# Squares of the new x summed on TensorE tile by tile, and element-wise work taken off GpSimd

## The chip, the cores and the metric

The kernel runs on one core of one Trainium2 chip. What is counted is device time in microseconds (us) of one execution, as the median of several runs. The engines are named as the profile names them: PE is TensorE's matrix product, PEld its weight load, DVE is VectorE, ACT is ScalarE, POOL is GpSimd, SP is the engine that issues most transfers.

## The reference

A decoder trunk of two layers, with 512 tokens and a width of 1024, all in f32. Layer 0 mixes with dilated attention and a state-space model (S5), layer 1 ("odd") with a gated linear recurrence. Each layer then has a gated feed-forward network (FFN) with 2816 hidden columns. Every one of the four sub-layers is put between two RMS norms:

```
for layer in range(2):
    hn  = rms_norm(x, norm_mix_pre[layer])
    mix = even_mixer(hn, ...) if layer == 0 else odd_mixer(hn, ...)
    x   = x + rms_norm(mix, norm_mix_post[layer])
    hn  = rms_norm(x, norm_ffn_pre[layer])
    ff  = (silu(hn @ w_gate) * (hn @ w_up)) @ w_down
    x   = x + rms_norm(ff, norm_ffn_post[layer])

rms_norm(x, g) = x * rsqrt(mean(x * x, axis=-1) + 1e-6) * g

odd_mixer: z = xn @ w_in; xc = conv4(z[:, :1024]) + bias
    gate_r, gate_i = sigmoid(xc @ w_r + b_r), sigmoid(xc @ w_i + b_i)   # blocks of 256
    log_a = -8 * gate_r * softplus(-lam)
    h[t]  = exp(log_a) * h[t-1] + sqrt(-expm1(2 * log_a)) * (gate_i * xc)
    y     = (h * gelu(z[:, 1024:])) @ w_out
```

## The kernel before

The activations lie transposed: x is eight tiles `xT[f]` of 128 channels by 512 tokens, and a product of a weight with x gives 128 output columns by 512 tokens in a PSUM bank. Each f32 operand is split into a high and a low part, so that one product is three matmuls: hi·hi, hi·lo and lo·hi (`mm3`, whose matmuls all carry line 170). The parts of a weight are `whi_` (a copy on ACT, line 240) and `wlo_` (a subtraction, line 241, on DVE unless `wrows` or `first_cols` is given another engine); those of the normed x are `xh_` (ACT, line 499) and `xl_` (DVE, line 487).

The sum over channels in a norm is a sum over partitions. `col_sums` takes it as matmuls with one column of ones: 128 tokens come out as one PSUM column. `rstd_of` turns the four columns into 1/rms: a scale on DVE (`rst`, line 378), a power on POOL (`rsy`, line 381), and, where the next norm wants it, `eps` on DVE (line 383). `bcast_sb` spreads the result over the partitions with four 128x128 matmuls (`bc`) and a copy into SBUF (`bcs`).

Four times the kernel goes through `out_proj`: products with an output matrix (`op_`), the RMS norm after it, and the addition to x. The tail of it runs by halves of 256 tokens (`norm_half`): for each f the output is scaled (line 492), added to `xT[f]` (DVE for f = 0, POOL for the others, lines 496 and 498), copied to `xh`, and subtracted for `xl`. Between these steps PE already makes the first four column blocks of the next stage (`half_cols`, banks `mo0b`, `fd0b`, `mo1b`) with x that is not yet divided by its rms. In this tail the order is pinned as it is written (`seq_of`, `pe.pin`). Everywhere else a scheduler at build time sets the order on each engine; on the chip an engine then runs its list in that order.

What the next stage needs is 1/rms of the new x, and this is `pre_rstd`: eight squares of whole tiles on ACT (`sq_`, line 423, two buffers), six additions into two accumulators `sqacc_` (line 425; f under 4 on DVE, the others on POOL), eight one-column products `cs_`, and `rstd_of`. In `ffn_up` the function `mid` calls it after the products of the first pair of columns that is built by a scheme with seven products over half tiles instead of eight (`product`; banks `f00b` to `f03b` with the pair's number at the end, 84 matmuls of 128x256 each; weight sums on DVE, lines 629 to 632; sums of x on DVE, lines 651 to 654, with hi and lo parts `th_`, `tl_`). The four early column blocks are copied out unscaled (line 614) and multiplied once the factor is there. In the odd layer `mid` runs while the first columns go through the convolution.

In the odd layer, per tile f: convolution with hi and lo (`ch`, `cl`, line 1512), gates (`gr`, `gi`, line 1541; `xc` times `gi` on POOL, line 1542), exp and tanh (`ga`, `gr`, lines 1549 and 1550), `lm` = `ga` squared on POOL (line 1556), `gr` (line 1557), a square root on ACT, `gr` times `xc`, the scan (line 1561), the gelu branch `gg` (lines 1574 to 1583; `gt` is its square, on POOL, line 1576), and `y1h`, `y1l` (line 1587), which the products `op_mo` of the odd layer read.

Of the kernel before, what the change touches and what calls it, by code (L numbers as in the profile page):

```python
# [94 lines left out]
def hybrid_trunk(  # L95
# [318 lines left out]
    def pre_rstd(nm, keep=None):  # L414
        accs = []
        for f in (0, 4, 1, 5, 2, 6, 3, 7):
            eng = dve if f < NF // 2 else pool
            if f % (NF // 2) == 0:
                accs.append(sb.tile([P, S], F32, tag="sqacc", bufs=2, name=f"sqacc_{nm}{f}"))
                act.activation(accs[-1], xT[f], AF.Square)  # L420
            else:
# [1 line left out]
                act.activation(q, xT[f], AF.Square)
# [1 line left out]
                eng.tensor_tensor(acc, acc, q, op=ALU.add)  # L425
        return rstd_of(col_sums(lambda t: [a[:, t * P:(t + 1) * P] for a in accs], 0, NT, nm, "mid"), NT, nm,
                       keep=keep)

    def out_proj(wget, ks, yh, yl, pname, layer, nm, otile, gname, glayer, ntail, tail_alloc, early, eng0=None,
# [42 lines left out]
        ready.clear()  # L472

        def norm_half(h):
# [15 lines left out]
            for f in range(NF):  # L490
# [8 lines left out]
                seq_of(act.activation(xh[f][:, HS[h]], xf, AF.Copy, scale=col(gname, glayer * NF + f)))  # L499
# [971 lines left out]
    def odd_body(xh, xl, first, lp):
# [52 lines left out]
        def gates(blk):  # L1524
# [4 lines left out]
            for n in range(2):  # L1529
# [12 lines left out]
                pool.tensor_tensor(xc[f], xc[f], t, op=ALU.mult)  # L1542
# [121 lines left out]
```

## Time and profile before

| | |
|---|---|
| median of 3 runs | 1211.34 us (1208.27 to 1212.36) |
| the profiled execution | 1211.84 us |
| its span in the trace | 1210.1 us |
| mean granted PE clock | 0.973 |
| POOL busy | 181.9 us, 173 instructions |

The trace shows the stages at about these times: attention and S5 to 200 us, out-projection of layer 0 with its norm to 293, FFN of layer 0 up to 513 and down to 642, its norm to 667, odd layer to 801, its out-projection with its norm to 854, FFN of layer 1 up to 1073, its down product to the end.

In the rows below, "128x512 f32 x8" is the shape of an instruction and how often it stands in the group. In rows of the timeline the first number is the start, the second the duration; several instructions may be merged into one row (x4). In square brackets is how long the engine was idle before it, and what it then came free on. In rows of a table of windows there are for each engine the busy time in the window and the number of instructions, then the granted clock of PE (1.00 is full), the share of the DMA engines that was busy, and GB/s.

### The profile page before, as it was taken

Reading aid. Unit: us, or ns where it says so; the run is one execution under the profiler, and the core shown is the slowest. Engines: PE = TensorE matmul, PEld = TensorE weight load, DVE = VectorE, ACT = ScalarE, POOL = GpSimd, SP = SyncE. Lnnn points to the kernel's source line nnn. Section 1 sums busy time; section 2 is a strip of 40 time slices with the busy share of each in tenths; the row PEclk is TensorE's granted clock in tenths of the full one; section 3 lists DMA queues with packets and bytes.
Section 4 is the critical chain, followed back from the end, with each engine's and each line's share of the span. In section 5 each row is a group of like instructions: output and inputs, shape, how many; then the busy total and the mean of one; then the engine's idle time right before and its main releaser. Section 6 shows DMA issues by size and latency. Waiting matters only on the chain.

```text
span 1210.1 us, 19987 instructions
## 1 busy us (share of the span) xinstructions
PE 1138.7 (94%) x7406; PEld 1012.8 (84%) x7406; DVE 905.5 (75%) x1823; ACT 622.9 (51%) x1255; POOL 181.9 (15%) x173
## 2 busy tenths in 40 slices
PE   7899999999699999999999999599799999999997
PEld 6787766888699999988889878389689999988886
DVE  7978775369789998983327897977989998894224
ACT  6555576448455545652334467354755455482222
POOL 2000020432400000000135045434310000000001
PEclk9899899999799999999999999799999999999999
DMA  8344410712233323332331223140243233343321
GB/s 207 103 137 128 110 47 1 192 36 70 70 96 105 89 79 105 107 108 94 120 96 36 87 88 105 53 135 6 69 122 97 84 100 89 105 131 105 97 69 70
DMA packets 165273, 113.44 MB, mean 94 GB/s; under 512 B 26820, under 2 KB 141752, under 8 KB 165176
## 3 DMA queue, kind: packets, MB, share of 16 engines
q1 hardware_dynamic: 161848, 109.94, 30.9%
q10 hardware_dynamic: 3040, 2.17, 0.7%
q8 instruction: 58, 0.95, 0.3%
q14 instruction: 39, 0.32, 0.1%
q0 software_dynamic: 288, 0.07, 0.0%
HBM read 103.75 MB, written 4.19 MB: 89 GB/s over the span
## 4 chain that ended last, share of the span: by engine, by line
PE 57%; DVE 6%; issue 5%; ACT 3%; DMA 3%; POOL 2%; SPq 0%; DVEq 0%; POOLq 0%; ACTq 0%
PE op_fd L170 10%; PE fo L170 10%; PE f00b L170 4%; PE f01b L170 4%; PE f02b L170 4%; PE f12b L170 4%; PE f10b L170 4%; PE f11b L170 4%; PE op_mo L170 2%; PE f03b L170 2%; PE f13b L170 2%; PE fd0b L170 2%; POOL sqacc_f L425 2%; PE xbb L170 2%; PE mo1b L170 1%
## 5 line engine op out<-in xcount | busy, mean ns | idle before, releaser
L241 DVE TENSOR_TENSOR wlo_fo<-wraw_fo,whi_fo 128x512 fp32r<-128x512 f32 x44 | 30.3, 691 | 64.0 <-PE fo L170 58.1
L170 PE MATMUL op_fd<-hi_f,whi_fd 128*128 128x512 f32 (+1 forms) x200 | 73.5, 368 | 0.0
L170 PE MATMUL op_fd<-lo_f,whi_fd 128*128 128x512 f32 (+1 forms) x200 | 73.2, 366 | 0.0
L170 PE MATMUL op_fd<-hi_f,wlo_fd 128*128 128x512 f32 (+1 forms) x200 | 72.9, 368 | 0.0
L241 DVE TENSOR_TENSOR wlo_fd<-wraw_fd,whi_fd 128x512 fp32r<-128x512 f32 x44 | 30.6, 705 | 55.2 <-ACT whi_fd L240 41.1
L170 PE MATMUL fo<-wlo_fo,hi_f 128*128 128x512 f32 x176 | 69.6, 396 | 0.0
L170 PE MATMUL fo<-whi_fo,lo_f 128*128 128x512 f32 x176 | 69.2, 394 | 0.0
L170 PE MATMUL fo<-whi_fo,hi_f 128*128 128x512 f32 x176 | 68.8, 395 | 0.0
L240 ACT ACTIVATE whi_fo<-wraw_fo 128x512 fp32r<-128x512 f32 x44 | 27.3, 631 | 71.4 <-DMA wraw_fo<-in_ffn_w_down_dram 45.1
L240 ACT ACTIVATE whi_fd<-wraw_fd 128x512 fp32r<-128x512 f32 x44 | 27.3, 630 | 56.4 <-DMA wraw_fd<-in_ffn_w_down_dram 36.4
L811 POOL TENSOR_SCALAR s<-ss,eps_f 128x1 f32<-128x1 f32 x4 | 1.1, 266 | 298.6 <-ACT fsq L809 298.6
L170 PE MATMUL op_mo<-y1l,whi_mo 128*128 128x256 f32 (+1 forms) x88 | 31.6, 361 | 13.2 <-DVE y1l L1587 13.2
L170 PE MATMUL qkv<-whi_qkv,xh_m 128*128 128x512 f32 x96 | 42.4, 443 | 1.3 <-DVE up L1196 1.0
L170 PEld LDWEIGHTS op_fd<-lo_f,whi_fd 128*128 128x128 f32 x200 | 37.7, 189 | 6.8
L170 PEld LDWEIGHTS op_fd<-hi_f,wlo_fd 128*128 128x128 f32 x200 | 37.7, 188 | 6.6
L170 PEld LDWEIGHTS op_fd<-hi_f,whi_fd 128*128 128x128 f32 x200 | 37.7, 188 | 6.4
L170 PE MATMUL qkv<-wlo_qkv,xh_m 128*128 128x512 f32 x96 | 39.3, 410 | 2.8 <-DVE wlo_qkv L241 2.8
L241 POOL TENSOR_TENSOR wlo_mo<-wraw_mo,whi_mo 128x512 fp32r<-128x512 f32 x22 | 34.0, 1576 | 50.1 <-ACT whi_mo L240 50.1
L453 POOL TENSOR_TENSOR oacc_fd<-oacc_fd,osq_fd 128x512 f32<-128x512 f32 x3 | 4.2, 1409 | 247.7 <-ACT osq_fd L452 247.6
L629 DVE TENSOR_TENSOR wraw_s_f<-wraw_f,wraw_f 128x512 f32<-128x512 f32 x40 | 27.5, 688 | 18.3 <-DMA wraw_f<-in_ffn_w_up_dram 14.1
L170 PEld LDWEIGHTS fo<-whi_fo,lo_f 128*128 128x128 f32 x176 | 33.1, 188 | 7.8
L170 PEld LDWEIGHTS fo<-whi_fo,hi_f 128*128 128x128 f32 x176 | 33.1, 188 | 7.8
(1987 smaller groups left out, 4482.7 us busy)
## 6 DMA issues: line engine op xcount, KB each, us to landing
wraw_f<-in_ffn_w_gate_dram SPq DMA_DIRECT2D x88, 256.0 KB, 3.2
wraw_f<-in_ffn_w_up_dram SPq DMA_DIRECT2D x88, 256.0 KB, 3.2
wraw_fd<-in_ffn_w_down_dram SPq DMA_DIRECT2D x44, 256.0 KB, 2.6
wraw_fo<-in_ffn_w_down_dram SPq DMA_DIRECT2D x44, 256.0 KB, 2.9
wraw_qkv<-in_ev_w_in_dram SPq DMA_DIRECT2D x24, 256.0 KB, 3.4
wraw_mo<-in_ev_w_out_dram SPq DMA_DIRECT2D x16, 256.0 KB, 4.9
wraw_xb<-in_od_w_in_dram SPq DMA_DIRECT2D x16, 256.0 KB, 3.2
wraw_gg<-in_od_w_in_dram SPq DMA_DIRECT2D x16, 256.0 KB, 3.0
```

The lines of the kernel that those rows point to most:

```text
L170: self.pin(nc.tensor.matmul(o, lhsT=lhsT, rhs=rhs, start=start, stop=stop, **kw))
L240: act.activation(hi, src, AF.Copy)
L241: eng.tensor_tensor(lo, src, hi.bitcast(F32), op=ALU.subtract)
L425: eng.tensor_tensor(acc, acc, q, op=ALU.add)
L453: pool.tensor_tensor(acc, acc, q, op=ALU.add)
L629: dve.tensor_tensor(s1, a21, a22, op=ALU.add)
L811: pool.tensor_scalar(s0, ss[:, 0:1], 1.0 / D, eps[:, t:t + 1], op0=ALU.mult, op1=ALU.add)
```

## The change

Three things change.

First, `pre_rstd` is gone. `norm_half` now squares each `xf` right after `xh`, by halves of 256 tokens (16 squares on ACT, `nsq_`), and `next_sums` adds them up on PE alone: for each half, f and block of 128 tokens one one-column f32 matmul, 32 in all, into one bank `nsum` (`ns_`), two tiles behind the ones being made. These matmuls are pinned between those of the early columns. The bank is taken from the six main ones for the tail and given back after it. This happens at three places: before FFN 0, before the odd layer, before FFN 1.

Second, in `ffn_up` `mid` is called right after the early columns have begun, so the first four blocks are multiplied as they leave PSUM.

Third, element-wise work moves from POOL: the additions of `osq` in `out_proj`, the 22 `wlo_mo`, the 8 `wlo_xb` and `xc` times `gi` to DVE; `lm` and `gt` to ACT as squares. The additions to `xT` and the power stay on POOL.

```diff
-    def pre_rstd(nm, keep=None):
-        accs = []
-        for f in (0, 4, 1, 5, 2, 6, 3, 7):
-            eng = dve if f < NF // 2 else pool
...
-                act.activation(q, xT[f], AF.Square)
-                acc = accs[f // (NF // 2)]
-                eng.tensor_tensor(acc, acc, q, op=ALU.add)
-        return rstd_of(col_sums(lambda t: [a[:, t * P:(t + 1) * P] for a in accs], 0, NT, nm, "mid"), NT, nm,
-                       keep=keep)
...
-                pool.tensor_tensor(acc, acc, q, op=ALU.add)
+                dve.tensor_tensor(acc, acc, q, op=ALU.add)
...
+        nb = sets["main"].pop(0)
+        share(next=(nb,))
+        nsum = bank(f"ns_{nm}", "next")
+
+        def next_sums(h, fs, q):
+            for i, f in enumerate(fs):
+                for t in range(2):
+                    c = 2 * h + t
+                    pe.pin(nc.tensor.matmul(nsum[:, c:c + 1], lhsT=q[:, i * HT + t * P:i * HT + (t + 1) * P],
+                                            rhs=ones[:, 0:1], start=(c == 0 and f == 0), stop=(f == NF - 1),
+                                            skip_group_check=True))
...
                 seq_of(act.activation(xh[f][:, HS[h]], xf, AF.Copy, scale=col(gname, glayer * NF + f)))
+                if f % 2 == 0:
+                    q = sb.tile([P, S], F32, tag="sqacc" if h else "sq", bufs=2, name=f"nsq_{nm}{h}{f}")
+                seq_of(act.activation(q[:, HS[f % 2]], xf, AF.Square))
                 late.append(f)
+                if f % 2 and f > 1:
+                    next_sums(h, (f - 3, f - 2), qlast)
+                if f % 2:
+                    qlast = q
...
+        sets["main"].insert(0, nb)
+        return xh, xl, (first, bs), nsum
...
-            env["rb"] = bcast_sb(pre_rstd(nm, eps), nm, "mid")
+            env["rb"] = bcast_sb(rstd_of(nsum[:, 0:NT], NT, nm, keep=eps), nm, "mid")
...
-                dve.tensor_copy(env[n][0], b)
+                dve.tensor_tensor(env[n][0], b, env["rb"], op=ALU.mult)
             else:
                 act.activation(env[n][1], b, AF.Copy)
+                gated(*env[n], n)
 
         heads = gemm_cols(cols2[:NFIRST], first, xh, xl, nm, evac)
         next(heads)
+        mid()
...
-            if n == NFIRST // 2:
-                mid()
-                for i in range(n):
-                    dve.tensor_tensor(env[i][0], env[i][0], env["rb"], op=ALU.mult)
-                    gated(*env[i], i)
...
-                        alloc, lambda: first_cols(ffn_cols(0), "f0"), pool)
+                        alloc, lambda: first_cols(ffn_cols(0), "f0"))
...
-                pool.tensor_tensor(xc[f], xc[f], t, op=ALU.mult)
+                dve.tensor_tensor(xc[f], xc[f], t, op=ALU.mult)
...
-                    pool.tensor_tensor(m, al[f], al[f], op=ALU.mult)
+                    act.activation(m, al[f], AF.Square)
...
-            pool.tensor_tensor(t, g, g, op=ALU.mult)
+            act.activation(t, g, AF.Square)
```

On PE, at the end of the early columns of layer 0's FFN, before the change, the product of the sums stood between matmuls of pairs 3 and 4 (the last digit of a bank's name before the underscore is the pair; the first pair built this way is 2):

```order
L170 MATMUL f02b3_3750<-xl_mo07_3001,whi_f03c_1_3732 128x256
L170 MATMUL f02b3_3750<-xh_mo07_2993,wlo_f03c_1_3733 128x256
L170 MATMUL f03b2_3552<-tl_f03_3534,whi_f02d_1_3461 128x256
L170 MATMUL f03b2_3552<-th_f03_3533,wlo_f02d_1_3462 128x256
L170 MATMUL cs_f0_3664<-ones_161,sqacc_f00_3642 128x1
L170 MATMUL f01b4_3897<-th_f00_3479,whi_f04b_0_3892 128x256
L170 MATMUL f01b4_3897<-tl_f00_3480,whi_f04b_0_3892 128x256
```

Now the spread of 1/rms (`bc_f0`) follows the last early column and stands ahead of the first product of the first pair:

```order
L170 MATMUL mo0b1_3160<-xl_mo07_3001,whi_f01_1_2958 128x256
L170 MATMUL mo0b2_3161<-xl_mo07_3001,whi_f02_1_2970 128x256
L170 MATMUL mo0b3_3162<-xl_mo07_3001,whi_f03_1_2982 128x256
L170 MATMUL bc_f0_3488<-cst_63,rsy_f0_3484 128x128 x4
L170 MATMUL f00b2_3624<-xh_mo00_2986,whi_f02a_0_3510 128x256
L170 MATMUL f00b2_3624<-xl_mo00_2994,whi_f02a_0_3510 128x256
```

Behind it everything PE does waits for `rsy_f0`; before, `bc_f0` stood inside pair 5. On DVE, in the same stage, the scale `rst_f0` stood between weight sums of pairs 5 and 7:

```order
L632 TENSOR_TENSOR wraw_s_f05_4_4010<-wraw_f050_4_4003,wraw_t_f05_0_4011 128x512
L710 TENSOR_TENSOR pu_f03_3752<-pu_f03_3752 128x256
L714 TENSOR_TENSOR pu_f03_3752<-pu_f03_3752,f02b3_3750 128x256
L378 TENSOR_SCALAR rst_f0_3673<-cs_f0_3664 128x4
L629 TENSOR_TENSOR wraw_s_f07_0_4305<-wraw_f071_0_4301,wraw_f071_4_4303 128x512
L383 TENSOR_SCALAR eps_f0_3329<-rst_f0_3673 128x4
L241 TENSOR_TENSOR wlo_f05c_1_4029<-wraw_s_f05_4_4010,whi_f05c_1_4028 128x512
```

Now it stands among the sums of x for the first pair (`wraw_tr_`), 31 rows ahead of the first multiplied column block:

```order
L661 TENSOR_TENSOR wraw_tr_f00_0_3542<-xb_f00_3539,xa_f00_3538 128x256
L662 TENSOR_TENSOR wraw_tr_f00_0_3542<-xb_f00_3539,wraw_tr_f00_2_3543 128x256
L660 TENSOR_TENSOR wraw_tr_f01_2_3561<-xa_f01_3556 128x256
L378 TENSOR_SCALAR rst_f0_3483<-ns_mo0_3002 128x4
L663 TENSOR_TENSOR wraw_tr_f00_2_3543<-wraw_tr_f00_0_3542,xb_f00_3539 128x256
L661 TENSOR_TENSOR wraw_tr_f01_0_3560<-xb_f01_3557,xa_f01_3556 128x256
L662 TENSOR_TENSOR wraw_tr_f01_0_3560<-xb_f01_3557,wraw_tr_f01_2_3561 128x256
L383 TENSOR_SCALAR eps_f0_3386<-rst_f0_3483 128x4
L241 TENSOR_TENSOR wlo_f02b_0_3535<-wraw_t_f02_0_3505,whi_f02b_0_3534 128x512
```

So `rst_f0` moved from the time of pair 3 to the preparation of pair 2. On ACT, in the odd layer's recurrence, the square roots followed the last tanh (`gr6`, `gr7`, line 1550) behind a table load:

```order
L1550 ACTIVATE gr6_8464<-gr6_8464,sp8_7833 128x512
L1550 ACTIVATE gr7_8483<-gr7_8483,sp8_7833 128x512
L1558 ACT_TABLE_LOAD
L1558 ACTIVATE gr0_8240<-gr0_8240 128x512
L1558 ACTIVATE gr1_8259<-gr1_8259 128x512
L240 ACTIVATE whi_gg7_1_8829<-wraw_gg7_4_8823 128x512
```

Now the squares `lm` stand there too (lines 1554, 1560 and 1562 are 1550, 1556 and 1558 of before):

```order
L1554 ACTIVATE gr6_8514<-gr6_8514,sp8_7914 128x512
L1554 ACTIVATE gr7_8533<-gr7_8533,sp8_7914 128x512
L1560 ACTIVATE lm0_8583<-ga0_8559 128x512
L1560 ACTIVATE lm1_8587<-ga1_8562 128x512
L240 ACTIVATE whi_gg7_1_8879<-wraw_gg7_4_8873 128x512
L240 ACTIVATE whi_gg7_0_8875<-wraw_gg7_0_8871 128x512
L1562 ACT_TABLE_LOAD
L1562 ACTIVATE gr0_8290<-gr0_8290 128x512
L1560 ACTIVATE lm2_8591<-ga2_8565 128x512
```

Each `lm` comes after the last tanh on ACT, where POOL could make it as soon as its `ga` was there.

More of the change, by code (lines that the diff above doesn't have):

```diff
@@ L527, in out_proj @@
         in_order[0] = False
-        return xh, xl, (first, bs)
+        sets["main"].insert(0, nb)
+        return xh, xl, (first, bs), nsum
     def rows_of(w):
@@ L583, in ffn_cols, with ffn_up @@
         return [(w[layer], n * P) for n in range(NH) for w in (ffn_w_gate, ffn_w_up)]
-    def ffn_up(layer, xh, xl, first, nm, hp):
+    def ffn_up(layer, xh, xl, first, nsum, nm, hp):
         cols2 = ffn_cols(layer)
@@ L739, in spare, with ffn @@
         return sb.tile([P, S], F32, tag="gt" if i < 2 else "ut", bufs=2, name=name)
-    def ffn(layer, xh, xl, first):
+    def ffn(layer, xh, xl, first, nsum):
         with tc.tile_pool(name=f"hid{layer}", bufs=1) as hp:
@@ L744, in ffn @@
             share(side=(6, 7))
-            hh, hl, eps = ffn_up(layer, xh, xl, first, f"f{layer}", hp)
+            hh, hl, eps = ffn_up(layer, xh, xl, first, nsum, f"f{layer}", hp)
             def otile(i, name):
@@ L757, in ffn, with ffn_last @@
             got = out_proj(rows_of(ffn_w_down[layer]), list(range(NH)), hh, hl, "p1", layer, f"fd{layer}", otile,
-                           "g0", layer + 1, 6, alloc, lambda: first_cols(odd_cols(), "xb", pool), eps=eps)
+                           "g0", layer + 1, 6, alloc, lambda: first_cols(odd_cols(), "xb"), eps=eps)
             places[:] = [p for p in places if p[0] is sb]
         return got
-    def ffn_last(xh, xl, first):
+    def ffn_last(xh, xl, first, nsum):
         hp = ctx.enter_context(tc.tile_pool(name="hid1", bufs=1))
@@ L765, in ffn_last @@
         share(side=(6, 7))
-        hh, hl, eps = ffn_up(1, xh, xl, first, "f1", hp)
+        hh, hl, eps = ffn_up(1, xh, xl, first, nsum, "f1", hp)
         xk = [None] * (2 * NT)
@@ L1460, in even_body, with odd_layer, odd_body @@
         return out_proj(wget, list(range(NF)), yh, yl, "p0", 0, "mo0", otile, "g1", 0, EV_TAIL,
-                        alloc, lambda: first_cols(ffn_cols(0), "f0"), pool)
+                        alloc, lambda: first_cols(ffn_cols(0), "f0"))
     def odd_cols():
         return [(od_w_in[0], f * P) for f in range(NF)]
-    def odd_layer(xh, xl, first):
+    def odd_layer(xh, xl, first, nsum):
         with tc.tile_pool(name="odd", bufs=1) as lp:
-            return odd_body(xh, xl, first, lp)
-    def odd_body(xh, xl, first, lp):
+            return odd_body(xh, xl, first, nsum, lp)
+    def odd_body(xh, xl, first, nsum, lp):
         w = od_w_in[0]
@@ L1498, in mid @@
         def mid():
-            env["rb"] = bcast_sb(pre_rstd("m1"), "m1", "mid")
+            env["rb"] = bcast_sb(rstd_of(nsum[:, 0:NT], NT, "m1"), "m1", "mid")
         def conv(f, b):
@@ L1618, in odd_body @@
         return out_proj(rows_of(od_w_out[0]), list(range(NF)), yh, yl, "p0", 1, "mo1", otile, "g1", 1, 6,
-                        alloc, lambda: first_cols(ffn_cols(1), "f1"), pool)
-    xh, xl, first = even_layer()
+                        alloc, lambda: first_cols(ffn_cols(1), "f1"))
+    xh, xl, first, nsum = even_layer()
     for f in range(NF):
         dump(f"x1_{f}", xT[f])
-    xh, xl, first = ffn(0, xh, xl, first)
+    xh, xl, first, nsum = ffn(0, xh, xl, first, nsum)
     for f in range(NF):
@@ L1628, in hybrid_trunk @@
         return
-    xh, xl, first = odd_layer(xh, xl, first)
+    xh, xl, first, nsum = odd_layer(xh, xl, first, nsum)
     for f in range(NF):
         dump(f"x3_{f}", xT[f])
-    ffn_last(xh, xl, first)
+    ffn_last(xh, xl, first, nsum)
 _INS = ['x', 'positions', 'norm_mix_pre', 'norm_mix_post', 'norm_ffn_pre', 'norm_ffn_post',
```

6 lines of the change are left out of this document (1 added, 5 removed).

## The prediction

> **What bounds the kernel now.** I read the page's busy shares first, then windows of 20 us for each stage, then the timeline where PE falls short.
>
> ```profile
> PE 1138.7 (94%) x7406; PEld 1012.8 (84%) x7406; DVE 905.5 (75%) x1823; ACT 622.9 (51%) x1255; POOL 181.9 (15%) x173
> 280.00:300.00 20.00, 18.92 (x154) 18.37 (x152) 19.70 (x43) 18.45 (x39) 4.04 (x5) 1.00 0.36 106
> 300.00:320.00 20.00, 12.35 (x69) 11.41 (x68) 16.25 (x31) 9.17 (x19) 10.36 (x2) 0.74 0.09 26
> 320.00:340.00 20.00, 17.01 (x115) 16.56 (x114) 13.66 (x24) 8.61 (x16) 3.50 (x3) 0.83 0.32 93
> 340.00:360.00 20.00, 17.92 (x151) 17.72 (x150) 18.64 (x39) 12.82 (x26) 0.00 (x0) 1.00 0.37 105
> 360.00:380.00 20.00, 20.00 (x170) 20.00 (x170) 20.00 (x41) 10.81 (x22) 0.00 (x0) 1.00 0.37 107
> 860.00:880.00 20.00, 12.87 (x76) 11.68 (x76) 17.59 (x34) 11.11 (x24) 10.76 (x2) 0.84 0.05 14
> 880.00:900.00 20.00, 17.49 (x136) 16.73 (x134) 15.12 (x29) 10.20 (x18) 2.65 (x3) 0.96 0.49 142
> ```
>
> PE is busy nearly everywhere, so the change can only pay where PE is not fed. Busy time understates the loss, since slow matmuls count as busy; the number of matmuls shows it better. In a full window of the FFN PE does 170 matmuls (360 to 380), one in 20/170 = 0.118 us. Right after the norm it does 69, 115 and 151, and in layer 1 76 and 136. The losses are 101 + 55 + 19 = 175 matmuls, 20.6 us, at FFN 0, and 94 + 34 = 128, 15.1 us, at FFN 1. The granted clock falls to 0.74 to 0.84 in the starved windows and is 1.00 in the full ones, so part of the loss is matmuls that run slowly after the wait.
>
> What starves PE there is seen in the timeline of the two stages:
>
> ```profile
> 302.76 9.46 POOL L425 TENSOR_TENSOR sqacc_f<-sqacc_f,sq_f 128x512 f32<-128x512 f32 x1 [18.72 <-issue]
> 309.81 0.68 DVE L631 TENSOR_TENSOR wraw_f<-wraw_f,wraw_f 128x512 f32<-128x512 f32 x1
> 310.42 0.68 DVE L241 TENSOR_TENSOR wlo_f04c<-wraw_s_f,whi_f04c 128x512 fp32r<-128x512 f32 x1
> 312.25 0.63 ACT L423 ACTIVATE sq_f<-xT 128x512 f32<-128x512 f32 x1 [7.85 <-POOL sqacc_f L425]
> 864.47 9.32 POOL L425 TENSOR_TENSOR sqacc_f<-sqacc_f,sq_f 128x512 f32<-128x512 f32 x1 [18.85 <-issue]
> 875.82 0.58 PE L170 MATMUL f12b<-xh_mo,whi_f12c 128*128 128x256 f32 x1 [5.57 <-ACT pv_f L696]
> ```
>
> One addition on POOL takes 9.46 us. It ends at 312.22, 1.1 us after a run of DVE subtractions and additions from SBUF that ends at 311.10 (310.42 + 0.68). ACT's next square waits 7.85 us for the buffer which that addition still reads; behind it in ACT's queue stand evacuations such as `pv_f`, and PE stands still for a bank (5.57 us in layer 1). Layer 1 has the same, with 9.32 us. So the chain is DVE, POOL, ACT, PE, and the change removes its POOL link.
>
> The Trainium skill, page "SBUF — State Buffer", section "Who interferes with whom", says that a DVE instruction with two SBUF inputs and a GpSimd instruction that reads SBUF exclude each other, the later one being blocked outright. The trace agrees in the 9.46 us. The rule also speaks against the change, at the power that stays on POOL: this is the first rival below.
>
> **The change, part by part.**
>
> *The square chain before FFN 0 and FFN 1.* The stall above goes. Not all 20.6 us come back, because other things are late next, and these two do not change: the weights' transfers, and DVE's work for the first pair.
>
> ```profile
> 320.70 4.30 DMA wraw_f<-in_ffn_w_up_dram
> 884.44 3.33 DMA wraw_f<-in_ffn_w_up_dram
> 887.79 0.63 ACT L240 ACTIVATE whi_f15d<-wraw_f 128x512 fp32r<-128x512 f32 x1 [4.18 <-DMA wraw_f<-in_ffn_w_up_dram]
> ```
>
> These transfers stand in the chain that ended last, 4.3 and 3.3 us. They were issued late since their buffers came free late, behind the same stall, so most of it should go with it. In the windows DVE is full from 280 to 300 (19.70) and must still make the sums and low parts of the first pair. What remains lost I estimate at 6 us at FFN 0, between 3 (only this start-up) and 10 (the two transfer waits and as much again), and at 4 us at FFN 1, between 3 and 8. So the stalls give back 20.6 − 6 = 14.6 us and 15.1 − 4 = 11.1 us before what is added.
>
> *The added column products.* The old ones (`cs_f`, 8 per place) go, 32 come. Their price is read where four of them stand in a row in the norm:
>
> ```profile
> 270.61 0.28 PE L170 MATMUL cs_mo<-ones,oacc_mo 128*128 128x1 f32 x2
> ...
> 271.19 0.36 PE L170 MATMUL cs_mo<-ones,oqs_mo 128*128 128x1 f32 x2
> 271.42 0.36 PE L170 MATMUL mo0b<-xh_mo,whi_f 128*128 128x256 f32 x1
> 267.70 0.74 PE L170 MATMUL mo0b<-xl_mo,whi_f 128*128 128x256 f32 x4 [0.34 <-DVE xl_mo L487]
> 268.83 0.39 PE L170 MATMUL mo0b<-xh_mo,whi_f 128*128 128x256 f32 x1 [0.39 <-ACT xh_mo L499]
> 680.00:700.00 20.00, 19.09 (x82) 14.90 (x81) 18.15 (x32) 12.44 (x19) 1.29 (x1) 1.00 0.28 85
> ```
>
> Four take 271.42 − 270.61 = 0.81 us (each leaves two records), 0.20 us each. Per place 32 × 0.20 − 8 × 0.20 = 4.9 us more on PE, in a stretch where PE already waits only 0.34 and 0.39 us at a time, so little of it is hidden. At three places that is 14.7 us; the waits of 0.34 and 0.39 cover up to 0.7 of each, which I leave as slack. FFN 0 thus gains 14.6 − 4.9 = 9.7, FFN 1 11.1 − 4.9 = 6.2. Before the odd layer there was no such stall: the 4.9 stand against what PE loses from 680 to 700, where 82 matmuls stand against 87 in a full window of that length (740 to 760, below), about 1.2 us; the rest, 3.7 us, arrives at the recurrence.
>
> *The odd layer.* Here DVE sets the end:
>
> ```profile
> 740.00:760.00 20.00, 20.00 (x87) 16.01 (x85) 20.00 (x20) 10.69 (x19) 13.13 (x9) 1.00 0.24 79
> 760.00:780.00 20.00, 8.92 (x29) 6.44 (x28) 20.00 (x21) 8.13 (x13) 9.26 (x7) 0.74 0.20 65
> 714.68 1.77 DVE L1512 TENSOR_TENSOR cl<-xc,ch 128x512 fp32r<-128x512 f32 x1
> 720.40 0.68 DVE L1512 TENSOR_TENSOR cl<-xc,ch 128x512 fp32r<-128x512 f32 x1
> L1542 POOL TENSOR_TENSOR xc<-xc,gi 128x512 f32<-128x512 f32 x8 | 12.9, 1626 | 31.5 <-ACT gi L1541 31.4
> 736.55 1.30 DVE L1557 SCALAR_TENSOR_TENSOR gr<-lm,gr 128x512 f32<-128x512 f32 x2
> 740.46 1.32 ACT L1550 ACTIVATE gr<-gr,sp 128x512 f32<-128x512 f32 x2
> 774.18 1.21 DVE L1561 TENSOR_TENSOR_SCAN xc<-ga,gr 128x512 f32<-128x512 f32 x1
> 782.78 0.68 DVE L1587 SCALAR_TENSOR_TENSOR y1l<-gg,y1h 128x512 fp32r<-128x512 f32 x1
> 783.51 0.79 PE L170 MATMUL op_mo<-y1l,whi_mo 128*128 128x512 f32 x1 [3.41 <-DVE y1l L1587]
> PE op_mo L170 <- DVE y1l L1587: 13.2, 2, 9.8
> ```
>
> From 740 to 780 DVE is busy all the time with 20 or 21 instructions in 20 us, against 41 in the FFN's window. The same subtraction takes 1.77 us beside POOL and 0.68 alone. PE waits 13.2 us for `y1l` in two pieces (9.8 and 3.41). Without POOL's work DVE's rows take about 0.60 from start to start (309.81 to 310.42 above is 0.61), the scan 1.2 (the row at 774.18). That relief is large, but the order spends it: `lm` on ACT now comes after all eight tanh, the last of which ends at 740.46 + 1.32 = 741.78. With the 3.7 us from above and 0.6 for the square, the first `gr` of line 1557 (before: 736.55) can start at about 746. From it to the third `y1l` there are 52 rows on DVE, eight of them scans: 8 × 1.2 + 44 × 0.60 = 36.0, and 0.6 for waits. That is 782.6, against 782.78 before. So the odd layer takes the 3.7 us in and gives nothing: −1 at most, from the eight multiplications of line 1542 that no longer run beside POOL. I take −0.5. Bounds: +4 (DVE does not speed up and the shift stays) and −8 (of the 13.2 us, 8 go).
>
> *Layer 0's `wlo_mo`, the `osq` additions, `wlo_xb`* go to DVE at 0.60 instead of POOL at 1.58:
>
> ```profile
> 220.00:240.00 20.00, 20.00 (x87) 16.12 (x86) 2.11 (x4) 6.89 (x13) 11.47 (x9) 1.00 0.82 214
> 600.00:620.00 20.00, 20.00 (x88) 16.17 (x87) 3.46 (x5) 6.10 (x10) 5.76 (x5) 1.00 0.49 149
> L241 POOL TENSOR_TENSOR wlo_mo<-wraw_mo,whi_mo 128x512 fp32r<-128x512 f32 x22 | 34.0, 1576 | 50.1 <-ACT whi_mo L240 50.1
> ```
>
> There PE is full (20.00 of 20) and DVE idle (2.11 and 3.46), so this costs and gains nothing; the cover is DVE's idle time, and 9 more rows of 0.60 in 20 us leave it below half. The 16 half squares per place on ACT replace eight whole ones.
>
> *The sum:* −9.7 − 6.2 − 0.5 = −16.4 us against the profiled execution's 1211.84, that is 1195.4. The median of the runs lies 0.5 lower than that execution, 1211.34; I say 1196.
>
> **Rivals.**
>
> *The power is held off by DVE.* `bc` now is first in PE's queue before the first pair, ACT's copy and DVE's multiplication follow it, so a held power stops all four engines.
>
> ```profile
> 892.33 0.17 DVE L383 TENSOR_SCALAR eps_f<-rst_f 128x4 f32<-128x4 f32 x1
> 892.38 1.01 POOL L381 TENSOR_TENSOR rsy_f<-rst_f,neghalf 128x4 f32<-128x4 f32 x1 [7.34 <-DVE rst_f L378]
> 892.59 0.69 DVE L241 TENSOR_TENSOR wlo_f15c<-wraw_s_f,whi_f15c 128x512 fp32r<-128x512 f32 x1
> ```
>
> For it: between the scale and the first multiplied block stand 30 rows on DVE, nearly all with two inputs from SBUF, and such a run held the addition for 9.46 us. Against it: before, the power began 0.05 us after the one-input `eps` row and ran beside the next subtraction. In the new order `eps` is the fourth row after the scale, so the power should wait about 1 us. If it waits for the end of DVE's run (30 rows, some 15 us at 0.5), PE loses what the early columns do not cover: I estimate 5 us at FFN 0 and 4 at FFN 1. 1195.4 + 9 = 1204 to 1205. By the skill's rule ("SBUF — State Buffer", the same section) the power would go in at the first DVE row with one SBUF input, which is `eps`, and the sum would stay at 1195.4.
>
> *The stall is only uncovered work.* DVE's start-up of pair 2 and the late transfers fill the place: then 10 and 8 us stay lost, and the transfers' 4.3 and 3.3 us are not within them but as before. The gains are 20.6 − 10 − 4.3 − 4.9 = 1.4 and 15.1 − 8 − 3.3 − 4.9 = −1.1, with 0.5 in the odd layer: that is 1211.0, no change at all; with half of it 1203. The full DVE window ahead of the stall speaks for it; against it, DVE's busy time falls to 16.25 of 20 while PE is stopped, so DVE has time to give.
>
> *The odd layer gains too.* PE's 13.2 us there shrink by 6 to 8: the 41 DVE rows from 740 to 780, some five of them scans, would take 28 us at the pace above instead of 40, and only eight of 0.60 (line 1542) come on before the products. That gives 1195.4 − 6.5 = 1189. Against it stands the late `lm`.
>
> *Slower: the pinned sums wait.* Each of the 24 calls of `next_sums` stands in PE's order between early columns and needs a square on ACT, which needs the addition on POOL. If each waits 0.9 us, 24 × 0.9 = 21.6, and 1195.4 + 21.6 = 1217. It decides from 16.4 / 24 = 0.68 us per call. Against it: the sums stand two tiles behind, and PE's waits in this place now are 0.34 and 0.39; for it: ACT has 18.45 us of work from 280 to 300, and the 16 squares stand in its queue ahead of the next `xh`.
>
> **How the numbers follow.** Chances: forecast (1190 to 1201) 0.52; power held (1202 to 1207) 0.12; stall only uncovered work (1203 to 1212) 0.14; odd layer gains too (1186 to 1190) 0.12; slower (1215 and over) 0.10. The predicted time is the forecast's, 1196. The range from 1187 to 1209 holds the forecast, the power and the most part of two others, and leaves out the slower rival, the flat end of the third and the edge of the fourth, together about 0.18. A measurement of this kernel tells 0.3%, 3.6 us, from no change, so faster means under 1207.7: forecast, odd layer, power and half of the third give 0.82; same is 0.08, slower 0.10.
>
> **What the profile after would show.** The first step is right if no row of POOL near either FFN start lasts over 3 us, and the window from 300 to 320 has over 130 matmuls instead of 69. The added products: 32 `ns_` rows per place, early columns 4 to 5 us longer. The odd layer: `cl` rows all at 0.68, the first `gr` of the squares' line at about 746 less what FFN 0 gained, PE's wait for `y1l` again near 13 us. The power: `rsy_f0` starts within 2 us of `rst_f0`. I would be wrong above all if the wait of PE moves to `bc` or to the sums `tl` of the first pair instead of going, or if PE's wait for `y1l` shrinks.

## The result and the profile after

The changed kernel takes 1190.2 us in the median of 4 runs (1187.42 to 1191.3) against 1211.01 us for the kernel before (4 runs). The ratio of the two is 0.9828, 95% interval 0.9802 to 0.9853. Measured again it took 1189.52 us, ratio 0.983 (0.9817 to 0.9844); every ratio is to the kernel before, measured beside it. The profiled execution after was the fastest of its kernel, 1187.42 us with a span of 1185.3; so its span is 24.8 us shorter than the one before, while the medians differ by 20.8 us.

The page's busy times and the windows at the places of the prediction, after the change:

```profile
PE 1134.0 (96%) x7550; PEld 1012.0 (85%) x7550; DVE 888.5 (75%) x1857; ACT 630.7 (53%) x1295; POOL 60.4 (5%) x101
280.00:300.00 20.00, 20.00 (x173) 20.00 (x171) 19.31 (x46) 17.53 (x39) 7.16 (x8) 1.00 0.33 93
300.00:320.00 20.00, 18.69 (x148) 17.62 (x146) 20.00 (x39) 15.68 (x33) 0.00 (x0) 1.00 0.29 82
320.00:340.00 20.00, 19.17 (x161) 19.17 (x162) 19.49 (x39) 11.65 (x24) 0.00 (x0) 1.00 0.40 115
840.00:860.00 20.00, 18.14 (x147) 17.49 (x146) 19.00 (x43) 19.27 (x39) 1.06 (x1) 1.00 0.28 79
860.00:880.00 20.00, 19.32 (x160) 18.90 (x159) 19.61 (x40) 10.03 (x21) 0.00 (x0) 1.00 0.52 150
880.00:900.00 20.00, 19.88 (x167) 19.68 (x166) 20.00 (x40) 11.50 (x23) 0.00 (x0) 1.00 0.37 106
```

POOL fell from 181.9 to 60.4 us. At the start of FFN 0 the windows now hold 148 and 161 matmuls where 69 and 115 stood, and the clock stays at 1.00 in them. What remains lost at FFN 0 from 300 to 340 is 22 + 9 = 31 matmuls of 0.118 us, 3.6 us. FFN 1 now begins at 846.1, so its start is in the three windows from 840 to 900: 23 + 10 + 3 = 36 matmuls are missing there, 4.2 us.

To see where the time came from, I take the first matmul of each stage (`mo0b`, `f00b`, `fd0b`, `xbb`, `mo1b`, `f10b`, and the last start of `fo`) in each trace. The lengths between these marks, in us:

| stage | before | changed | difference |
|---|---|---|---|
| norm ahead of FFN 0 (`mo0b` to `f00b`) | 25.7 | 33.7 | +8.0 |
| FFN 0 (to `fd0b`) | 350.3 | 330.2 | −20.1 |
| norm ahead of the odd layer (to `xbb`) | 24.5 | 32.1 | +7.6 |
| odd layer and its out-projection (to `mo1b`) | 161.9 | 151.7 | −10.2 |
| norm ahead of FFN 1 (to `f10b`) | 24.4 | 32.2 | +7.8 |
| FFN 1 (to the last `fo`) | 350.2 | 332.4 | −17.8 |

Each norm became longer and the stage behind it became shorter by more. The price of the sums can be read on PE, in the timeline of the norm:

```profile
275.84 0.95 PE L468 MATMUL ns_mo<-ones,nsq_mo 128*128 128x1 f32 x8
276.65 0.48 PE L170 MATMUL mo0b<-xl_mo,whi_f 128*128 128x256 f32 x2
PE mo0b L170 <- DVE xl_mo L485: 0.7, 1, 0.7
PE ns_mo L468 <- ACT nsq_mo L500: 0.4, 1, 0.4
```

Four products (two records each) take 276.65 − 275.84 = 0.81 us, and the second pair of rows, from the waits of the norm ahead of FFN 0, shows that PE waited 0.4 us in all for a square. 32 × 0.20 = 6.5, and with the four `bc` matmuls (some 1 us), which moved from the FFN or the odd layer into the norm, this is the 7.6 to 8.0 us of the table.

The odd layer, from three timelines of the changed kernel:

```profile
733.02 1.29 DVE L1561 SCALAR_TENSOR_TENSOR gr<-lm,gr 128x512 f32<-128x512 f32 x2 [0.97 <-ACT lm L1560]
768.93 0.69 DVE L1591 SCALAR_TENSOR_TENSOR y1l<-gg,y1h 128x512 fp32r<-128x512 f32 x1
767.92 2.07 PE L170 MATMUL op_mo<-y1h,whi_mo 128*128 128x512 f32 x4 [9.56 <-ACT y1h L1590]
760.00:780.00 20.00, 12.08 (x46) 9.52 (x47) 20.00 (x33) 12.90 (x24) 0.00 (x0) 0.74 0.18 58
```

DVE does 33 instructions in the window from 760 to 780 instead of 21, and is still full. PE waits 9.56 us once where it waited 9.84 and 3.41.

### The profile page after: what moved, and what is told of

Its sections match the earlier page's. It is cut to its first block, busy times and chain, and to the rows that moved or that the text cites. A ratio compares the mean times of both kernels' runs of the same rounds, so it can differ in the third digit from the quotient of the medians.

```text
span 1185.3 us, 20265 instructions
## 1 busy us (share of the span) xinstructions
PE 1134.0 (96%) x7550; PEld 1012.0 (85%) x7550; DVE 888.5 (75%) x1857; ACT 630.7 (53%) x1295; POOL 60.4 (5%) x101
## 4 chain that ended last, share of the span: by engine, by line
PE 70%; ACT 9%; DVE 8%; DMA 7%; issue 3%; POOL 1%; SPq 0%; ACTq 0%; DVEq 0%; POOLq 0%
PE fo L170 10%; PE op_fd L170 10%; PE f02b L170 5%; PE f01b L170 4%; PE f00b L170 4%; PE f11b L170 4%; PE qkv L170 4%; PE f12b L170 4%; PE f10b L170 4%; PE op_mo L170 3%; PE f03b L170 2%; PE f13b L170 2%; PE rg L170 2%; PE xbb L170 2%; PE fd0b L170 2%
## 5 line engine op out<-in xcount | busy, mean ns | idle before, releaser
L241 DVE TENSOR_TENSOR wlo_fo<-wraw_fo,whi_fo 128x512 fp32r<-128x512 f32 x44 | 30.3, 691 | 63.7 <-PE fo L170 58.8
L170 PEld LDWEIGHTS fo<-wlo_fo,hi_f 128*128 128x128 f32 x176 | 33.1, 188 | 7.5
L170 PE MATMUL op_mo<-y1h,whi_mo 128*128 128x256 f32 (+1 forms) x88 | 28.6, 352 | 11.0 <-ACT y1h L1590 9.6
L170 PE MATMUL qkv<-whi_qkv,xl_m 128*128 128x512 f32 x96 | 39.1, 407 | 0.0
L241 DVE TENSOR_TENSOR wlo_mo<-wraw_mo,whi_mo 128x512 fp32r<-128x512 f32 x32 | 21.5, 687 | 14.8 <-ACT whi_mo L240 14.7
```

Of the source, the lines that this page charges most:

```text
L170: self.pin(nc.tensor.matmul(o, lhsT=lhsT, rhs=rhs, start=start, stop=stop, **kw))
L241: eng.tensor_tensor(lo, src, hi.bitcast(F32), op=ALU.subtract)
```

## The experiments

The table has the lengths of the stages for all of them, by the same marks, one profiled execution each. The medians stand with each experiment. The two traces of the changed kernel agree within 0.6 us in every stage. The time ahead of the first mark is not in the table; over all traces it varies from 263.3 to 268.6 us, so differences of stages do not add up to those of the medians.

| | norm 0 | FFN 0 | norm odd | odd layer | norm 1 | FFN 1 |
|---|---|---|---|---|---|---|
| before | 25.7 | 350.3 | 24.5 | 161.9 | 24.4 | 350.2 |
| changed | 33.7 | 330.2 | 32.1 | 151.7 | 32.2 | 332.4 |
| changed_again | 33.8 | 330.2 | 32.1 | 152.3 | 32.2 | 332.6 |
| sums_only | 39.8 | 330.0 | 32.0 | 159.0 | 32.1 | 331.6 |
| pool_only | 25.7 | 348.5 | 24.5 | 156.2 | 24.3 | 352.6 |
| adds_dve | 25.3 | 345.3 | 26.1 | 159.7 | 24.3 | 348.9 |
| adds_dve_pool_only | 25.7 | 345.1 | 26.1 | 151.4 | 24.4 | 347.9 |
| late_mid | 34.5 | 334.5 | 32.1 | 151.6 | 31.4 | 336.5 |
| lm_back | 33.7 | 330.2 | 32.1 | 153.1 | 32.1 | 332.1 |
| odd_back | 33.8 | 330.6 | 32.1 | 155.5 | 32.1 | 332.2 |
| ns_twice | 45.0 | 325.5 | 42.1 | 152.3 | 42.2 | 329.3 |
| ns_quarter | 30.0 | 334.8 | 25.9 | 157.7 | 26.0 | 332.9 |
| ns_f32r | 30.3 | 331.0 | 30.1 | 153.3 | 30.0 | 334.5 |
| ns_f32r_again | 30.3 | 331.8 | 31.5 | 155.0 | 29.9 | 334.6 |

**The two halves of the change.** `sums_only` is the changed kernel with the four edits on `osq`, `wlo_mo`, `wlo_xb`, and the three of the odd layer undone. `pool_only` is the kernel before with only these.

```diff
-                dve.tensor_tensor(acc, acc, q, op=ALU.add)
+                pool.tensor_tensor(acc, acc, q, op=ALU.add)
...
-                dve.tensor_tensor(xc[f], xc[f], t, op=ALU.mult)
+                pool.tensor_tensor(xc[f], xc[f], t, op=ALU.mult)
...
-                    act.activation(m, al[f], AF.Square)
+                    pool.tensor_tensor(m, al[f], al[f], op=ALU.mult)
...
```

> The changed kernel with its third part undone: squares of the new x summed by PE and early 1/rms, but osq additions, wlo_mo, wlo_xb, xc times gi, lm and gt on GpSimd as before. Theory: the two FFN starts keep their whole gain (20.1 and 17.8 us between the marks of the two traces) and the one-column products their whole price (7.6 to 8.0 us per norm), and only the odd layer's 6.5 us go back: about 1190.2 + 6.5 = 1197 us. Rival: the GpSimd work also held up the FFN starts or the norms, then 1205 or more; or the odd layer's gain came from the earlier 1/rms and not from GpSimd, then 1190.

> The kernel before with only the third part (element-wise work off GpSimd; pre_rstd stays, its three additions per norm on GpSimd too). Theory: the stalls at the FFN starts stay, since the accumulating addition on GpSimd (9.46 and 9.32 us) stays; the odd layer gains about 6.5: 1204 to 1205 us, with a POOL row of over 5 us still at both FFN starts. Rival: with less other work on GpSimd the addition gets in earlier and the stall goes too: 1190 or less.

`sums_only` took 1198.1 us, ratio 0.9901 (0.9874 to 0.9927); `pool_only` 1204.68 us, ratio 0.9957 (0.9939 to 0.9975), both as the theory said. With the sums alone both FFN stages have their whole gain (330.0 and 331.6), and the odd layer loses 7.3. The relief of GpSimd is worth 7.9 us by this median (1198.1 − 1190.2) and 5.6 by that of `pool_only` (1210.28 for the kernel before, beside it). With GpSimd relieved alone the FFN stages stay where they were, and the stall on POOL stays; this is the answer of its trace on the accumulators:

```profile
L425 POOL TENSOR_TENSOR sqacc_f<-sqacc_f,sq_f x6: 1549/1833/9545, 300.8 to 877.7; 128x512 f32<-128x512 f32 x6
```

(least, median and greatest duration in ns: the longest is 9.5 us.) In `sums_only` PE waits 13.2 us for `y1l` again, as before:

```profile
L170 PE MATMUL op_mo<-y1l,whi_mo 128*128 128x256 f32 (+1 forms) x88 | 31.7, 362 | 13.2 <-DVE y1l L1591 13.2
264.00:284.00 20.00, 18.99 (x108) 18.68 (x107) 7.72 (x19) 6.83 (x19) 6.53 (x8) 0.66 0.00 1
```

Its norm 0 is 6 us longer than the changed kernel's, but not by waiting: the second row shows a granted clock of 0.66 over those 20 us, with PE 18.99 us busy on only 108 matmuls.

**Is the addition on POOL the stall?** In the kernel before I put all additions of squares on DVE, and in a second version did the same with the third part of the change.

```diff
-            eng = dve if f < NF // 2 else pool
+            eng = dve
```

> The kernel before with one word changed: all six additions of squares of pre_rstd on DVE, none on GpSimd; no one-column products added, 1/rms as late as before. Theory (the stall is the GpSimd addition held out by DVE's two-input rows): both stalls go without the price of the sums, 1211 less 20 to 30: 1182 to 1191 us. Rival (a chain of squares through two buffers in the middle of the start-up stalls ACT and PE whoever adds, and it is the place of the sums that matters): 1202 to 1211.

> The kernel before with the third part and with all additions of pre_rstd on DVE, without the sums on PE. Theory: as the one with the additions on DVE alone, less the 6.5 us of the odd layer: 1176 to 1185 us, which would beat the changed kernel, since it has no one-column products. Rival (place of the sums matters): 1196 to 1205.

The first took 1204.54 us, ratio 0.9947 (0.9929 to 0.9964): the rival's size, not the theory's. FFN 0 went from 350.3 to 345.3, and FFN 1 from 350.2 to 348.9, so the addition on POOL was worth 5.0 and 1.3 us there, not 20.6 and 15.1; by the medians it was worth 5.7 in all. Its windows, its waits on PE and its additions:

```profile
300.00:320.00 20.00, 12.99 (x85) 11.93 (x84) 20.00 (x39) 12.56 (x24) 0.00 (x0) 0.90 0.24 67
320.00:340.00 20.00, 17.52 (x124) 17.23 (x124) 14.23 (x30) 9.20 (x16) 1.01 (x1) 0.84 0.37 105
PE f01b L170 <- DVE pu_f L712: 4.1, 1, 4.1
PE f00b L170 <- DVE gt_f L711: 2.1, 1, 2.1
L425 DVE TENSOR_TENSOR sqacc_f<-sqacc_f,sq_f x12: 678/692/714, 299.9 to 879.5; 128x512 f32<-128x512 f32 x12
```

No addition takes more than 0.71 us and POOL does nothing from 300 to 320, yet PE makes 85 matmuls there, with DVE at 20.00 of 20. With the stall on POOL gone, DVE's own list was late next. PE waits 4.1 us for `pu_f` and 2.1 us for `gt_f`, results that DVE makes from the first pairs' banks. Line 711 (`gt`) needs 1/rms, and its first row starts at 337.49 us, after the factor's copy `bcs` at 332.49.

The second took 1192.89 us, ratio 0.9856 (0.9827 to 0.9885), between the two expectations: the odd layer gained as with the changed kernel (151.4), the FFN stages as in the first. It is 2.7 us above the changed kernel's first median, with norms that are 6 to 8 us shorter. The two intervals overlap (0.9827 to 0.9885 against 0.9802 to 0.9853), so it is not shown that the sums on PE are worth more than the additions on DVE. By the traces the changed kernel is 6.9 and 7.7 us ahead in FFN 0 and FFN 1 together with their norms, and 6.3 us behind in the odd layer with its norm (183.8 against 177.5): there the sums in the norm only cost.

**Place of the sums or place of 1/rms?** Squares and sums stay in the norm; `mid` and the scaling of the early blocks go back behind the first pair.

```diff
-                dve.tensor_tensor(env[n][0], b, env["rb"], op=ALU.mult)
+                dve.tensor_copy(env[n][0], b)
...
-                gated(*env[n], n)
...
         next(heads)
-        mid()
...
+            if n == NFIRST // 2:
+                mid()
+                for i in range(n):
+                    dve.tensor_tensor(env[i][0], env[i][0], env["rb"], op=ALU.mult)
+                    gated(*env[i], i)
```

> The changed kernel with the squares and sums in the norm as they are, but 1/rms, its spread and the scaling of the four early column blocks put back behind the first pair's products, as before. Theory A (what the stall was is the chain of squares and additions itself): no change, 1189 to 1192 us. Theory B (the banks of the first pairs cannot be evacuated before the factor is there, and DVE's list is reordered around it): 3 to 6 us come back at each FFN start: 1196 to 1202.

1194.29 us, ratio 0.987 (0.985 to 0.989), between the two forecasts. The two FFN stages are 4.3 and 4.1 us longer than in the changed kernel, the size of theory B, but not for its reason: the edit moves `mid` back in the program, and the scheduler at build time brought the factor forward again. The copy `bcs` of the factor stands here in the changed kernel, in `late_mid` and in `adds_dve`:

```profile
302.43 0.59 ACT L405 ACTIVATE bcs_f<-bc_f 128x512 f32<-128x512 f32 x1
304.67 0.58 ACT L405 ACTIVATE bcs_f<-bc_f 128x512 f32<-128x512 f32 x1
332.49 0.60 ACT L405 ACTIVATE bcs_f<-bc_f 128x512 f32<-128x512 f32 x1 [0.43 <-PE bc_f L170]
```

That is 2.5, 4.4 and 40.8 us after the first matmul of FFN 0. So `late_mid` does not test a late factor. It tests another order of the lists, with a copy and a multiplication where the changed kernel has one row. PE waits 3.3 us for `whi_f03c`, which on ACT comes behind `whi_f05d`, and that waits for a transfer; the granted clock dips there again:

```profile
320.00:340.00 20.00, 18.02 (x130) 18.02 (x131) 19.28 (x40) 9.29 (x19) 0.00 (x0) 0.83 0.41 119
PE f02b L170 <- ACT whi_f03c L240: 3.3, 1, 3.3
320.78 0.63 ACT L240 ACTIVATE whi_f05d<-wraw_f 128x512 fp32r<-128x512 f32 x1 [2.19 <-DMA wraw_f<-in_ffn_w_up_dram]
```

FFN 0's 20.1 us can be told apart by edits, not by causes: 5.0 for the addition on POOL (`adds_dve`); 10.8 more when all squares and additions leave the FFN's start and the factor comes 36 us earlier in it (345.3 to 334.5); 4.3 more for the place of `mid` and the order that follows from it (334.5 to 330.2). Together with the norm ahead, the second step is only 1.6 us (370.6 to 369.0), since the sums lengthen the norm, and the third is 5.1 (to 363.9). No run has the sums in the norm and the factor late, so the two parts of the second step stay untold.

**What the sums cost.** Each product of the sums twice; one quarter of them, which leaves six of eight tiles out of the sum; and each with squares rounded to fp32r, the rounded f32 type of the `whi` and `xh` tiles, which leaves one record per product in the trace instead of two ("one pass").

```diff
 # ns_twice: after each product
+                    pe.pin(nc.tensor.matmul(nsum[:, 8 + c:9 + c], lhsT=q[:, i * HT + t * P:i * HT + (t + 1) * P],
+                                            rhs=ones[:, 0:1], start=False, stop=(f == NF - 1),
+                                            skip_group_check=True))
 # ns_quarter
-                for t in range(2):
+                for t in range(2 if f < 2 else 0):
...
 # ns_f32r
...
-                                            rhs=ones[:, 0:1], start=(c == 0 and f == 0), stop=(f == NF - 1),
+                                            rhs=ones_r[:, 0:2], start=(c == 0 and f == 0), stop=(f == NF - 1),
...
-                    q = sb.tile([P, S], F32, tag="sqacc" if h else "sq", bufs=2, name=f"nsq_{nm}{h}{f}")
+                    q = sb.tile([P, S], F32R, tag="sqacc" if h else "sq", bufs=2, name=f"nsq_{nm}{h}{f}")
...
```

> The changed kernel with each one-column product of the squares issued twice (the second into unused columns): 32 more per norm, 0.20 us each, 6.5 us per norm, 19.5 in all. If PE's time in the norms is paid in full: 1190.2 + 19.5 = 1210 us. Rival (the two FFN starts are bound by DVE's and ACT's preparation, which runs ahead while PE is held up in the norm, so that a longer norm is given back): the two FFN places cost 2 to 4 each and the odd layer's 4 to 6.5: 1199 to 1204.

> The changed kernel with the column products of the first two of eight tiles only: 8 per norm instead of 32; the sum of squares leaves the other six tiles out, all squares on ACT stay. 24 products of 0.20 us less, 4.9 us per norm. Paid in full: 1190.2 - 14.6 = 1175.6 us. Rival (the long norm gives DVE and ACT a lead for the FFN start, as the doubled products gave back 4.7 and 2.9 us there): the FFN stages grow by 1.5 to 3 us each, 1178 to 1182.

> The changed kernel with the squares rounded to fp32r when ACT writes them, so that each product of the sums is one pass over PE instead of two (two columns of ones, the second unused). Each should take 0.10 to 0.12 us instead of 0.20, 3 us less per norm. Paid in full: 1190.2 - 9 = 1181 us. Rival (the FFN starts are bound by DVE's preparation): the time comes back as a wait at both FFN starts and only the place before the odd layer gains: 1186 to 1188.

`ns_twice` took 1221.56 us, ratio 1.0079 (1.0054 to 1.0103), with runs from 1210.52 to 1225.44; its profiled execution was at the low end. The norms are 10.0 to 11.3 us longer, not 6.5, and two rows of windows say why:

```profile
286.00:306.00 20.00, 20.00 (x148) 20.00 (x148) 19.24 (x46) 18.38 (x41) 6.92 (x7) 0.83 0.28 81
656.00:676.00 20.00, 20.00 (x148) 20.00 (x148) 10.79 (x49) 6.16 (x14) 5.38 (x7) 0.83 0.18 52
```

The clock falls to 0.83 in the norms. Neither expectation had that. The rival's part is there too: FFN 0 and FFN 1 became 4.7 and 3.1 us shorter, to 325.5 and 329.3. Since the price itself came out higher, the median lies above both forecasts.

`ns_quarter` took 1179.26 us, ratio 0.9748 (0.9726 to 0.977), the rival's range: 10.3 us less than the changed kernel measured beside it (1189.52) for 14.6 us of products. The stages did not do what the rival said, 1.5 to 3 us more for each FFN. In the trace norm 0 is 3.7 us shorter (with a granted clock of 0.91 from 264 to 284) and FFN 0 is 4.6 longer: nothing gained there. In the odd layer the 6.2 us of the norm are gone as well (157.7 against 151.7), though in that case also by the clock. Its window from 800 to 820 has 0.83 and 136 matmuls, where the changed kernel has 1.00 and 159; the one from 760 to 780 is no slower than the changed kernel's, 0.84 against 0.74:

```profile
760.00:780.00 20.00, 19.27 (x72) 15.26 (x73) 16.81 (x29) 11.62 (x21) 0.00 (x0) 0.84 0.34 105
800.00:820.00 20.00, 19.38 (x136) 19.21 (x137) 10.50 (x27) 7.99 (x21) 7.42 (x9) 0.83 0.01 1
```

Only FFN 1 kept it (norm −6.2, FFN +0.5). The stages of this trace add up to 5.0 us less than the changed kernel's, so half of the 10.3 us is not seen in them.

`ns_f32r` took 1187.18 us, ratio 0.9805 (0.9778 to 0.9832), in the rival's range. It was run again beside the changed kernel:

> The changed kernel as it is, beside the others of this call on one chip: 1188 to 1192 us.

> The version with one-pass sums once more, beside the changed kernel on one chip: if the first comparison holds, 3 us less than the changed kernel, 1185 to 1188; if the FFN starts take it all back, the same.

The changed kernel took 1189.52, the version with one pass 1188.63 us, ratio 0.9818 (0.9801 to 0.9835). The intervals overlap. The norms are 2.0 to 3.4 us shorter in the first trace and 0.6 to 3.5 in the second, and the stages behind them 0.8 to 2.7 us longer. Whether it is faster than the changed kernel stays open; if so, by 1 to 3 us.

**What carries the odd layer.** Only `lm` back on GpSimd; then `xc` times `gi`, `lm` and `gt` back together.

```diff
-                    act.activation(m, al[f], AF.Square)
+                    pool.tensor_tensor(m, al[f], al[f], op=ALU.mult)
```

> The changed kernel with only lm, the square of ga, back on GpSimd. Theory of the prediction (lm on ACT stands behind all tanh and delays the first gr by some 9 us, which spends DVE's relief): the first gr comes earlier again, PE's wait for y1 shrinks by 3 to 6 us: 1184 to 1187. Rival (GpSimd beside DVE costs more than the late start, since each instruction shuts the other out): 1191 to 1196.

> The changed kernel with xc times gi, lm and gt (the odd layer's 24 instructions) back on GpSimd; wlo_mo, wlo_xb and the osq additions stay on DVE. Theory (these 24 carry the odd layer's gain, through DVE's pace): the whole 6.5 to 7.9 us go back, 1196 to 1198. Rival (wlo_mo, ten of which run on GpSimd in the middle of the recurrence, carries it): 1190 to 1193.

`lm_back` took 1190.02 us, ratio 0.9837 (0.9816 to 0.9859): no difference, and neither expectation. The first `gr` came 6.3 us earlier than in the changed kernel (726.71 against 733.02), as the theory said, but PE got nothing from it:

```profile
726.71 1.30 DVE L1561 SCALAR_TENSOR_TENSOR gr<-lm,gr 128x512 f32<-128x512 f32 x2
755.72 0.68 DVE L1591 SCALAR_TENSOR_TENSOR y1l<-gg,y1h 128x512 fp32r<-128x512 f32 x1
L170 PE MATMUL op_mo<-y1l,whi_mo 128*128 128x512 f32 (+1 forms) x64 | 23.6, 369 | 6.1 <-DVE y1l L1591 6.1
```

The first `y1l` came at 755.72, where the changed kernel's came at 748.3. `odd_back` took 1191.8 us, ratio 0.9849 (0.9831 to 0.9866), in its rival's range and 2.3 us above the changed kernel beside it, with intervals that overlap. In the traces the odd layer is 3.8 us longer than in the changed kernel (155.5), and 3.5 us shorter than in `sums_only` (159.0), where the `wlo_mo`, `wlo_xb` and `osq` work is on POOL too. So by these marks the three groups of the odd layer and the rest carry about half each of the 7.3 us; by the medians the three groups carry 2.3 of 7.9.

## Why the prediction was right or wrong

The time lies in the range, on the forecast side: 1190.2 measured against 1196, a gain of 20.8 where 15 to 16 was said, at the edge between the forecast's own range and the case that the odd layer gains too. By the stages of the traces the gain is 24.7 us, 4 more than by the medians, so the single steps below are no surer than that. That the time came near is partly luck: the reading on which the forecast stood, that one link is the whole loss, did not hold, and the change took away more than that link. Step by step:

- **"The chain is DVE, POOL, ACT, PE, and the change removes its POOL link."** The link was there, but it was not most of the loss. `adds_dve` removed it and nothing else and got 5.0 and 1.3 us of the 20.6 and 15.1. What then held PE was DVE's list at the FFN start and the late factor, seen only once the POOL row was gone. The prediction saw this rival ("the stall is only uncovered work") and gave it 0.14; as a reading of the link it was the better one, as a forecast of the change it was not, since the change also takes the additions out of DVE's list there and brings the factor early.
- **What stays lost, 6 and 4 us.** Too much at FFN 0, where 3.6 us are left by the count of matmuls, and right at FFN 1 with 4.2. FFN 0 with its norm gained 12.1 us, not 9.7, which is this difference of 2.4.
- **The loss before, 15.1 us at FFN 1.** Too small. It was counted from 860 on, but FFN 1 begins at 853.0 in the kernel before, and the windows on both sides are short of 170 too:

```profile
840.00:860.00 20.00, 18.66 (x142) 17.97 (x141) 19.71 (x44) 17.58 (x36) 5.14 (x6) 0.95 0.33 95
900.00:920.00 20.00, 19.66 (x165) 19.66 (x166) 19.63 (x41) 12.62 (x27) 0.00 (x0) 1.00 0.37 106
```

  With them 28 + 94 + 34 + 5 = 161 matmuls are missing, 19.0 us. The prediction's own sum then gives 19.0 − 4.2 − 4.9 = 9.9 us for FFN 1 with its norm; measured are 10.0, where 6.2 was said. At FFN 0 the window from 280 to 300 (154) would add 1.9 us in the same way and put that sum 1.9 too high, so the count is no surer than 2 us. The clock in the starved windows was read as 0.74 to 0.84; the one from 880 to 900 has 0.96.
- **A longer norm gives the FFN a lead.** This is not in the prediction. FFN 0 took 334.8, 330.2 and 325.5 us behind norms of 30.0, 33.7 and 45.0 (`ns_quarter`, changed, `ns_twice`), which fits DVE and ACT preparing the first pair while PE is held in the norm. At FFN 1 `ns_twice` shows it with 3.1 us, `ns_quarter` hardly (0.5).
- **The price of the sums, 0.20 us each.** Right as a duration (0.81 us for four). The norms grew by 7.6 to 8.0, of which `bc` is 1.05; that is more than the 4 to 5 us given as a sign, since the 8 old products stood in the stage behind and not in the norm. As a cost to the kernel it was too high: 24 products of 32 taken out per norm would be 14.6 us, and gave about 10.
- **3.7 us arrive at the odd layer's recurrence.** Right: at `fd0b` the changed trace is 12.1 us ahead, at the last `gg` 759.8 − 751.6 = 8.2, so 3.9 arrived.
- **The odd layer gives nothing net, −0.5.** From `fd0b` to `mo1b` it is 186.4 before and 183.8 after, −2.6. The times that I worked out came true: the first `gr` at 746 − 12.1 = 733.9, measured 733.02; the third `y1l` at 782.6 − 12.1 = 770.5, measured 768.93. What was too small is the worth of the relief: with the sums but without it (`sums_only`) the same stretch takes 191.0, so it is 7.2 us, where the forecast counted 3.7 + 0.5 = 4.2 and the rival 6 to 8. PE's wait shrank from 13.2 us to 9.56 once, where 13 was said again, and by the prediction's own sign this step was wrong. That the late `lm` spends the relief is not borne out: `lm_back`, with the `gr` 6.3 us earlier, takes the same time. But it also puts GpSimd beside DVE again and has another order on DVE, so the price of the late `lm` alone is not shown. DVE's list is full from 740 to 780 in both (20.00 of 20 in each window).
- **The work of layer 0 moved to DVE costs nothing.** Right as far as the marks of `pool_only` show: norm 0 25.7, as before.
- **The power held off by DVE** did not happen. In the changed kernel it begins 0.31 us after the start of the scale:

```profile
293.09 0.16 DVE L378 TENSOR_SCALAR rst_f<-ns_mo 128x4 f32<-128x4 f32 x1
293.17 0.41 DVE L663 TENSOR_TENSOR wraw_tr_f<-wraw_tr_f,xb_f 128x256 f32<-128x256 f32 x1
293.40 1.06 POOL L381 TENSOR_TENSOR rsy_f<-rst_f,neghalf 128x4 f32<-128x4 f32 x1 [6.53 <-DVE rst_f L378]
294.18 0.16 DVE L383 TENSOR_SCALAR eps_f<-rst_f 128x4 f32<-128x4 f32 x1
```

  It is done by 294.46, 4.7 us before `bc` stands first on PE. By the Trainium skill, page "SBUF — State Buffer", section "Who interferes with whom", it could go on only beside a DVE row with at most one SBUF input that is not in a 2-port mode; it starts while a row with two runs and ends 0.28 us after the start of the `eps` row, so this trace fits the rule only if the row's start is not the start of its reading, which no run here tells.
- **The pinned sums wait** did not happen: 0.4 us in norm 0.

## What to carry to other kernels

A long instruction that ends a chain of waits is not yet what the time is lost to: count what the other engines still have to do in that window, and take the link away by itself before giving it the whole loss. Count the loss from the first instruction of the stage to the first full window, not in the windows that look worst. Where the stage behind is bound by preparation on DVE and ACT, work added to PE ahead of it can cost less than its duration, because the preparation gets a lead; at FFN 0 taking such work out gave nothing. Moving a reduction into the stage that makes its inputs empties the crowded start behind it and brings the result early, but its price falls due in the stage ahead: judge both together, place by place. By the traces it paid here at the two FFN starts and cost 6.3 us at the odd layer, against the additions on DVE. And where a scheduler orders the lists, look in the trace whether an edit moved what it was meant to move.

## What the runs showed of the hardware

The granted clock dips in stretches where PE hardly waits: to 0.83 in `ns_twice`'s norms, with PE busy 20.00 of 20 and 148 matmuls in a window that held 165 to 173 in the changed kernel, and to 0.66 in norm 0 of `sums_only`, where it cost 6 us in one execution. The Trainium skill, page "TensorE: Matmul & The Clock Gate", Part 1, says that the clock is gated by how busy PE has been recently. The dips in all three norms of `ns_twice` would fit that, if one-column products count as little work; `sums_only` and `late_mid` (0.91 from 266 to 286) have the same products in norm 0 as the changed kernel, though, and dipped where that did not. No run here was made for this, and what sets off such a dip stays open. It makes single traces differ by up to 6 us in a stage, so lengths of stages from one trace each carry that uncertainty, and the small differences of the table (under 2 us) are not shown.
